# Hybrid attention block: projections in another order, keeping split and later, a third score bank, and key halves copied by DMA

## The chip, the core and the metric

The kernel runs on one core of one Trainium2 chip. The metric is the device time of one execution in microseconds (us); where several executions were timed, their median. TensorE is called PE (PEld is its weight load), VectorE DVE, ScalarE ACT, GpSimd POOL, and SyncE SP. SP issues all the kernel's DMAs.

## What is computed

A decoder trunk of two layers over 512 tokens of width 1024, in float32. Each layer projects its input into fifteen parts for three groups of heads, runs the attention of each group, projects the result back, and then runs a gated MLP with a short convolution.

```python
def fox_attention(q, k, v, log_f):            # 4 heads, causal, S = 512
    ...
        s = jnp.einsum('bqhd,bkhd->bhqk', qb, k) * ATTN_SCALE
        s = s + c_q - c_k                     # c = cumsum(log_f)
        p, _ = masked_softmax(s, kpos[None, :] <= qpos[:, None])
    ...
def nsa_attention(q, kc, vc, ks, vs, kw, vw, gates, ...):   # 8 query heads, 2 key/value groups
    k_cmp = nsa_compress(kc, cmp_pos_k, cmp_w1_k, cmp_w2_k)
    v_cmp = nsa_compress(vc, cmp_pos_v, cmp_w1_v, cmp_w2_v)
    ...
        o = gb[..., 0:1] * o_c + gb[..., 1:2] * o_s + gb[..., 2:3] * o_w
    ...
def dilated_attention(q, k, v):               # 4 heads, three (window, dilation) patterns
    ...
def hybrid_mixer(h, cos, sin, w_in, ...):
    proj = h @ w_in
    (fq, fk, fv, ff, nq, kc, vc, ks, vs, kw, vw, ng, dq, dk, dv) = jnp.split(proj, splits, axis=-1)
    ...
    rope = lambda t, n: partial_rope(heads(t, n), cos, sin)   # nq, kc, ks, kw, dq, dk
    ...
    return mix @ w_out
def conv_ffn(h, w_up, conv_w, conv_b, w_down):
    u = h @ w_up                              # then a causal depthwise convolution of width 3
    ...
    return (jax.nn.silu(a) * b) @ w_down
def reference(x, positions, ...):             # x (1, 512, 1024) float32, 2 layers
    for l in range(DEPTH):
        h = rms_norm(x, attn_pre_norm[l])
        x = x + rms_norm(hybrid_mixer(h, ...), attn_post_norm[l])
        h = rms_norm(x, ffn_pre_norm[l])
        x = x + rms_norm(conv_ffn(h, ...), ffn_post_norm[l])
    return x
```

## The kernel before, in words

**Precision.** Every float32 operand of a matmul is held as two parts, a rounded high part and the rest, both in the type float32r. A product takes three matmuls (high by high, high by low, low by high). So each weight that is loaded is split: `part_weights` lets ACT copy the high part (line 144) and lets DVE (152) or POOL (148, for the names in `ONPOOL`) subtract for the low part. `mm` (line 113) is the helper that issues every matmul except transposes, so one line stands for nearly all of PE's work, and one goes by tile names.

**Weights.** `plan` lists the weight chunks in the order of use. `getw` loads two chunks ahead (`AHEAD`), and splits one ahead (`PRE`) in the attention part. The raw, high and low buffers have three slots each, so the load of a chunk waits on SP until the split three chunks earlier has read its slot, and a split waits until PE has done the chunk three earlier.

**PSUM.** Eight banks of 128x512 float32 carry names: acc (three: projections, compression, output sums), s (two: scores), o (one: attention output), pt (two: transposes). `ps(tag)` takes the next free bank of a name; PE waits at the first matmul into it until the readers of the old tile are done.

**The attention part** is one loop over 96 units plus 7 slots. A unit is one block of 128 queries of one head and branch: 16 units for FoX (group "f"), 64 for NSA ("n", 8 heads by two branches, selected and window, by 4 blocks), 16 for the dilated heads ("d"). Each unit runs through stages at fixed lags (`LAGS`): the score matmuls at lag 0 (`st_scores`), the masked row maximum on DVE (`st_max`, line 1084), the exponential on ACT (`st_exp`, 1089), the normalization on POOL (`st_norm`, 1096), the transposes on PE (`st_turn`, 1107), the split of the transposed block on ACT and DVE (1124, 1129), the value matmuls at lag 7, and the output. Blocks 0 and 1 of a head share one score bank.

**The filler.** Between units the loop calls `step()`, which advances the generator `main_pieces` by one piece: a quarter of a 128-column projection (`projT`, 6 matmuls of 512 columns), an eighth of a 256-column one (`proj256`, 12 matmuls of 256), a quarter of the compression MLP (`hidden`), and so on. The budget is 5 steps ahead of the loop, then 1.4 steps a unit for 12 units, and 0.8 after. `pieces.later(d, fn, ...)` puts work off by d steps. `operands(u)` calls `until(key, n)`: where a unit needs a query or key tile that has not been kept yet, the loop makes steps until it has. PE's order is this program order, written out by hand; the order on the other engines, SP too, is chosen by the framework's scheduler.

**Order of projections before:** kc (two chunks: compression keys and values, turned into windows), ks, sv, nq0 (two chunks, query heads 0 to 3), kw merged with the first compression MLP, nq1 (two chunks, heads 4 to 7) merged with the second, dv, dq, dk, and then the first half of the output projection. `merge(a, b)` takes two pieces of a and one of b in turn.

**Keeping.** One step after a projection chunk ends, `keep` runs `rope`: DVE shuffles the bank and multiplies it by the cosine (464, 465), POOL multiplies by the sine and adds (466, 467). The rotated tile lies in SBUF. `EV[3]` steps later `keep2` makes the operands: for a query pair `q_evac` (ACT 474, DVE 475, twice), for keys `k_evac` (ACT 486 four times, DVE 488 four times). A key tile holds the high part in its first half of columns and the low part in the second, and the same 64 rows twice, in both halves of the partitions; before, ACT and DVE write both copies.

**At the head of a layer** the FoX keys and values are projected (`pk_` holds the keys in two acc banks), then `fq_proj(0)` and `fq_proj(1)`, then the prefix sums of the log forget gates (`pcs`, matmuls with `utri`, line 598), and then the loop begins with kc; all of these use acc banks.

**The compression chain** (`cmp_pieces`) runs beside the loop, one part per unit, from the end of the second compression MLP: it takes banks of the name `CT` for two transposes, for the compressed keys and values, for four score tiles and for four transposes (line 1004).

**The FFN** uses all eight banks by name in turn (`tg`, `dacc`, `X8`).

## Time and profile before

| What | Value |
|---|---|
| Runs shown: lowest, median, highest | 1411.82, 1412.58, 1418.45 us |
| The profiled execution's own time | 1416.81 us |
| Its span, first to last instruction | 1415.0 us |
| Busy: PE, PEld, DVE, ACT, POOL | 94%, 81%, 63%, 51%, 27% |
| Granted clock of TensorE, mean | 0.986 |
| DMA | 123.67 MB, 161962 packets, mean 87 GB/s |

All durations come from the one profiled execution, and times are counted from the start of its span. Busy times are unions of instruction spans. Matmuls are pipelined and their ends are modelled, so the difference of two starts is what one of them took. An idle time before an instruction is given with what ended it, inferred from semaphores. Layer 0's attention loop lies at about 60 to 340 us of the span, layer 1's at about 757 to 1035.

### The profile page before, as it was taken

How to read it: one execution, taken by the hardware profiler on the slowest of the kernel's cores; microseconds unless marked ns; L12 is line 12 of the kernel's file. 1: busy time of each engine (PE TensorE's matmuls, PEld its weight loads, DVE VectorE, ACT ScalarE, POOL GpSimd, SP SyncE). 2: the span in 40 equal slices, each digit the busy share in tenths (PEclk: the TensorE clock that was granted, in tenths of full speed). 3: DMA queues.
4: the chain of work that ended last, by engine and by line, in shares of the span. 5: the costliest groups of instructions: out<-in, count | busy, mean ns of one | idle time of the engine just before them, and what ended most of it. 6: DMA issues, size and time to landing. Idle time of an engine off the chain costs nothing.

```text
span 1415.0 us, 19975 instructions
## 1 busy us (share of the span) xinstructions
PE 1337.1 (94%) x7291; PEld 1151.2 (81%) x7291; DVE 892.9 (63%) x1867; ACT 725.6 (51%) x1469; POOL 377.6 (27%) x409
## 2 busy tenths in 40 slices
PE   6987999998999999999999988989989999999997
PEld 5876887887888888888887878979878888888886
DVE  7767878877655555533476687787686555554334
ACT  5656675775543333332374667677754333333322
POOL 2385576545000000000006657654440000000000
PEclk9999999999999999999999989999999999999999
DMA  6222321123233333323423132202313333323231
GB/s 175 76 60 75 99 71 31 46 75 119 66 99 96 98 96 98 96 98 111 119 90 90 60 105 75 60 31 69 112 60 89 91 103 91 103 91 104 90 120 59
DMA packets 161962, 123.67 MB, mean 87 GB/s; under 512 B 8329, under 2 KB 152137, under 8 KB 161865
## 3 DMA queue, kind: packets, MB, share of 16 engines
q1 hardware_dynamic: 161864, 122.40, 28.8%
q8 instruction: 57, 0.93, 0.3%
q14 instruction: 41, 0.33, 0.1%
HBM read 118.19 MB, written 4.19 MB: 86 GB/s over the span
## 4 chain that ended last, share of the span: by engine, by line
PE 70%; DVE 12%; ACT 7%; POOL 6%; issue 3%; DMA 1%; SPq 0%; POOLq 0%; DVEq 0%; ACTq 0%
PE acc L113 31%; PE s L113 16%; PE pt L113 12%; PE o L113 9%; PE pt L1107 2%; DVE k L488 1%; POOL r L467 1%; DVE q L475 1%; DVE wl_w L152 1%; POOL r L466 1%; ACT r L1089 1%; POOL wt L781 1%; DVE x L308 1%; DVE hl L274 1%; DVE pl L1129 1%
## 5 line engine op out<-in xcount | busy, mean ns | idle before, releaser
L152 DVE TENSOR_TENSOR wl_up<-raw_up,wh_up 128x1024 fp32r<-128x1024 f32 x78 | 95.5, 1225 | 163.2 <-ACT wh_up L144 163.2
L144 ACT ACTIVATE wh_up<-raw_up 128x1024 fp32r<-128x1024 f32 (+1 forms) x90 | 89.4, 1002 | 154.1 <-PE acc L113 67.9
L152 DVE TENSOR_TENSOR wl_wd<-raw_wd,wh_wd 128x1024 fp32r<-128x1024 f32 x42 | 51.5, 1225 | 133.5 <-ACT wh_wd L144 133.5
L113 PE MATMUL s<-k,q 128*128 128x512 f32 (+3 forms) x384 | 100.6, 343 | 23.8 <-DVE sm L1084 8.3
L148 POOL TENSOR_TENSOR wl_kc<-raw_kc,wh_kc 128x512 fp32r<-128x512 f32 x8 | 12.2, 1546 | 411.1 <-ACT wh_kc L144 411.1
L144 ACT ACTIVATE wh_wd<-raw_wd 128x1024 fp32r<-128x1024 f32 x42 | 44.5, 1060 | 144.5 <-PE pt L113 135.5
L1089 ACT ACTIVATE r<-r,sm 128x128 f32<-128x128 f32 x192 | 106.8, 557 | 19.7 <-DVE sm L1084 18.8
L1096 POOL TENSOR_SCALAR r<-r,sm,gates 128x128 f32<-128x128 f32 (+3 forms) x128 | 86.2, 680 | 88.0 <-DVE sm L1094 48.1
L113 PE MATMUL acc<-hh,wh_up 128*128 128x512 f32 (+1 forms) x272 | 102.4, 376 | 0.0
L113 PE MATMUL acc<-hl,wh_up 128*128 128x512 f32 (+1 forms) x272 | 102.4, 376 | 0.0
L113 PE MATMUL acc<-hh,wl_up 128*128 128x512 f32 (+1 forms) x272 | 102.4, 376 | 0.0
L113 PEld LDWEIGHTS s<-k,q 128*128 128x128 f32 x384 | 65.0, 198 | 36.0 <-DVE sm L1084 11.8
L1129 DVE TENSOR_TENSOR pl<-pt,ph 128x384 fp32r<-128x384 f32 x144 | 85.2, 593 | 13.0 <-ACT ph L1124 11.9
L1124 ACT ACTIVATE ph<-pt 128x384 fp32r<-128x384 f32 x144 | 74.4, 518 | 34.9 <-PE pt L1107 33.8
L1107 PE MATMUL pt<-ident,r 128*128 128x128 f32 x480 | 80.1, 283 | 7.7 <-POOL r L1096 4.9
L1084 DVE CUSTOM_DVE_ANT_0 r<-s,cmask 128x128 f32<-128x128 f32 (+3 forms) x160 | 74.8, 481 | 17.4 <-PE s L113 15.3
L113 PE MATMUL acc<-wh_wd,gh 128*128 128x512 f32 x252 | 83.7, 389 | 0.0
L113 PE MATMUL s<-hh,wh_up 128*128 128x512 f32 (+1 forms) x224 | 80.6, 360 | 0.9 <-DVE hl L274 0.9
L113 PE MATMUL s<-hl,wh_up 128*128 128x512 f32 (+1 forms) x224 | 80.3, 359 | 0.0
L113 PE MATMUL s<-hh,wl_up 128*128 128x512 f32 (+1 forms) x224 | 80.3, 359 | 0.0
L113 PE MATMUL o<-ph,v 128*128 128x256 f32 (+1 forms) x288 | 72.8, 279 | 0.8 <-DVE mx L1165 0.8
L113 PE MATMUL o<-pl,v 128*128 128x256 f32 (+1 forms) x288 | 70.0, 290 | 1.7 <-DVE pl L1129 1.7
(434 smaller groups left out, 4023.4 us busy)
## 6 DMA issues: line engine op xcount, KB each, us to landing
raw_up<-in_w_up_dram SPq DMA_DIRECT2D x88, 512.0 KB, 3.8
raw_wd<-in_w_down_dram SPq DMA_DIRECT2D x44, 512.0 KB, 3.4
raw_wo<-in_w_out_dram SPq DMA_DIRECT2D x16, 512.0 KB, 3.5
x<-in_x_dram SPq DMA_DIRECT2D x8, 512.0 KB, 5.7
raw_nq<-in_w_in_dram SPq DMA_DIRECT2D x8, 512.0 KB, 3.8
raw_w<-in_cmp_w_k_dram SPq DMA_DIRECT2D x8, 512.0 KB, 4.0
raw_w<-in_cmp_w_v_dram SPq DMA_DIRECT2D x8, 512.0 KB, 3.8
raw_fk<-in_w_in_dram SPq DMA_DIRECT2D x4, 512.0 KB, 4.8
```

The costliest lines, as they stand in the source:

```text
L113: nc.tensor.matmul(o, lhsT=lhsT, rhs=rhs, start=start, stop=stop, skip_group_check=True)
L144: nc.scalar.activation(hi[:, ks], raw[:, ks], AF.Copy)
L152: nc.vector.tensor_sub(lo[:, ks], raw[:, ks], f(hi)[:, ks])
L274: nc.vector.scalar_tensor_tensor(lo, src, gain[:, k:k + 1], f(hi), op0=ALU.mult, op1=ALU.subtract)
L308: nc.vector.scalar_tensor_tensor(xs[s][:, cs], hs[s][:, cs], stats["r", s // 2][:, j:j + 1], xs[s][:, cs], op0=ALU.mult, op1=ALU.add)
L466: nc.gpsimd.tensor_mul(w, w, sinT)
L1084: nc.vector.tensor_tensor_reduce(row[:, 0:n], u["S"][:, 0:n], u["mask"][:, 512 - n:512], op0=ALU.add, op1=ALU.min, scale=1.0, scalar=3.0e3 ...
L1089: nc.scalar.activation(row[:, 0:n], row[:, 0:n], AF.Exp, scale=-1.0, bias=sm_[:, 0:1], accum_out=sm_[:, 1:2])
L1096: nc.gpsimd.tensor_scalar(row[:, 0:n], row[:, 0:n], sm_[:, 2:3], g_, op0=ALU.mult, op1=ALU.mult)
L1107: nc.tensor.transpose(p[:, 128 * b:128 * b + 128], src, ident)
L1124: nc.scalar.activation(hi, src, AF.Copy)
L1129: nc.vector.tensor_sub(*u["lo"])
```

## The change

Five things are changed together.

- **Order.** nq0 is one chunk now (query heads 0 and 1) and comes, with kw, ahead of sv. nq1 (heads 2 and 3) is merged with the first compression MLP, nq2 and nq3 (heads 4 to 7), one after the other (`both`), with the second. The plan of weights follows.
- **Keeping.** `EV[3]` goes from 1 to 2, and a query or key tile's two halves are made in two different steps.
- **Banks.** acc goes from three to two, s from two to three; where three acc banks were named together, one name becomes s, and the compression chain (`CT`) uses s.
- **Copies.** In `one_k` ACT and DVE write a key tile's rows once, and a DMA on SP's queue copies the 64 rows of 4 KB to the other half of the partitions. The FoX keys (`k_evac`) stay as they were.
- **Rows.** `NROW`, the number of row buffers of 128x512, goes from 10 to 12.

```diff
--- before.py
+++ after.py
@@ -24,22 +24,22 @@
             0.00027424818836152554, 5.3182957344688475e-05, 1.0313385246263351e-05)
 NST = 4
 NBIG = 24
-NROW = 10
+NROW = 12
 LAGS = (1, 2, 4, 5, 7, 7)
 TAIL = 4
-ONPOOL = ("sv", "dv", "dq", "dk", "ks", "nq0", "kw", "kc", "nq1",
+ONPOOL = ("sv", "dv", "dq", "dk", "ks", "nq0", "kw", "kc", "nq1", "nq2", "nq3",
           (0, "fk", 0), (0, "fk", 1), ("up", 0, 1), ("up", 0, 2), ("up", 0, 3), ("up", 1, 0))
 PRE = 1
 HCUT = ((0, 2), (2, 4))
 WGAP = 1
 CL = (1, 3, 5, 6)
-OT = (("acc", "acc"), ("acc", "s"), ("s", "o"), ("acc", "acc"))
+OT = (("acc", "acc"), ("s", "s"), ("s", "o"), ("acc", "acc"))
 PCUT = ((0, 2), (2, 4))
 X8 = "acc"
-CT = "acc"
+CT = "s"
 FIRST = 5
 DCUTS = ("w1", "wo")
-EV = (1, 3, 1, 1)
+EV = (1, 3, 1, 2)
 ORDER = (0, 1, 2, 4, 3, 5, 6, 7, 8)
 GM1 = ((0, 0), (0, 1), (1, 0), (1, 1), (2, 0), (2, 1), (3, 0), (3, 1))
 HA0 = (1, 3)
@@ -87,7 +87,7 @@
     small = ctx.enter_context(tc.tile_pool(name="small", bufs=8))
     psum = ctx.enter_context(tc.tile_pool(name="psum", bufs=1, space=PS))
     dram = ctx.enter_context(tc.tile_pool(name="dram", bufs=1, space=bass.MemoryType.DRAM))
-    PSB = {"acc": 3, "o": 1, "s": 2, "pt": 2}
+    PSB = {"acc": 2, "o": 1, "s": 3, "pt": 2}
     uid = [0]
 
     def nm(p):
@@ -177,15 +177,16 @@
         turned("fq", C_FQ, C_FQ + 128)
         turned("kc", C_KC, C_KC + 128)
         turned("ks", C_KC + 256)
+        turned("nq0", C_NQ)
+        turned("kw", C_KW)
         for c in range(2):
             ks = slice(4 * c, 4 * c + 4)
             plan.append(((l, "sv", c), [(wi[:, ks, C_KC + 384:C_KC + 512], 0, 0), (wi[:, ks, C_KW + 128:C_KW + 256], 0, 128)],
                          4, 256, False))
-        turned("nq0", C_NQ, C_NQ + 128)
-        for kv, starts in enumerate(((C_KW,), (C_NQ + 256, C_NQ + 384))):
+        for kv in range(2):
             for c in range(2):
-                if c < len(starts):
-                    plan.append(((l, ("kw", "nq1")[kv], c), [(wi[:, :, starts[c]:starts[c] + 128], 0, 0)], 8, 128, False))
+                if kv or c == 0:
+                    turned("nq%d" % (1 + kv + c), C_NQ + 128 * (1 + kv + c))
                 for d in range(2):
                     k0 = 8 * c + 4 * d
                     plan.append(((l, "w1", kv, 2 * c + d), [(w1s[kv][:, k0:k0 + 4, :], 0, 0)], 4, 256, False))
@@ -467,26 +468,30 @@
             nc.gpsimd.tensor_add(r, r, w)
             return r
 
+        def q_half(q, p, j):
+            src = p[64 * j:64 * j + 64, :]
+            nc.scalar.activation(q[0:64, j, :], src, AF.Copy, scale=-0.125)
+            nc.vector.scalar_tensor_tensor(q[64:128, j, :], src, -0.125, f(q[0:64, j, :]),
+                                           op0=ALU.mult, op1=ALU.subtract)
+
+        def k_half(k, p, j):
+
+            src = p[64 * j:64 * j + 64, :]
+            for u in (j, 1 - j):
+                nc.scalar.activation(k[64 * u:64 * u + 64, 0, :], src, AF.Copy)
+            for u in (j, 1 - j):
+                nc.vector.tensor_sub(k[64 * u:64 * u + 64, 1, :], src, f(k[64 * j:64 * j + 64, 0, :]))
+
         def q_evac(p):
             q = bt([128, 2, 512], F32R, "q")
             for j in range(2):
-                src = p[64 * j:64 * j + 64, :]
-                nc.scalar.activation(q[0:64, j, :], src, AF.Copy, scale=-0.125)
-                nc.vector.scalar_tensor_tensor(q[64:128, j, :], src, -0.125, f(q[0:64, j, :]),
-                                               op0=ALU.mult, op1=ALU.subtract)
+                q_half(q, p, j)
             return q
 
         def k_evac(p):
-
-            ks = []
+            ks = [bt([128, 2, 512], F32R, "k") for j in range(2)]
             for j in range(2):
-                k = bt([128, 2, 512], F32R, "k")
-                src = p[64 * j:64 * j + 64, :]
-                for u in (j, 1 - j):
-                    nc.scalar.activation(k[64 * u:64 * u + 64, 0, :], src, AF.Copy)
-                for u in (j, 1 - j):
-                    nc.vector.tensor_sub(k[64 * u:64 * u + 64, 1, :], src, f(k[64 * j:64 * j + 64, 0, :]))
-                ks.append(k)
+                k_half(ks[j], p, j)
             return ks
 
         def new_v():
@@ -509,7 +514,7 @@
         row_bcast(bias[:, 4:28], b_nsa_gate[l])
         zz = small.tile([128, NST, 28], F32, tag="zz", bufs=1, name=nm("zz"))
         wv = [getw(l, "fv", c, ahead=1) for c in range(3)]
-        pk_ = [ps("acc"), ps("acc")]
+        pk_ = [ps("acc"), ps("s")]
         fv = [new_v(), new_v()]
         tmode = tc.manual_schedule(engines={mybir.EngineType.PE})
         tmode.__enter__()
@@ -717,10 +722,26 @@
                     yield
 
         def keep(p, key):
-            pieces.later(EV[3], keep2, rope(p), key)
-
-        def keep2(r, key):
-            store.setdefault(key, []).extend([q_evac(r)] if key[-1] == "q" else k_evac(r))
+            r = rope(p)
+            if key[-1] == "q":
+                q = bt([128, 2, 512], F32R, "q")
+                pieces.later(EV[3], q_half, q, r, 0)
+                pieces.later(EV[3] + 1, last_q, key, q, r)
+            else:
+                pieces.later(EV[3], one_k, key, r, 0)
+                pieces.later(EV[3] + 1, one_k, key, r, 1)
+
+        def last_q(key, q, r):
+            q_half(q, r, 1)
+            store.setdefault(key, []).append(q)
+
+        def one_k(key, r, j):
+            k = bt([128, 2, 512], F32R, "k")
+            own, other = (slice(64 * u, 64 * u + 64) for u in (j, 1 - j))
+            nc.scalar.activation(k[own, 0, :], r[own, :], AF.Copy)
+            nc.vector.tensor_sub(k[own, 1, :], r[own, :], f(k[own, 0, :]))
+            nc.sync.dma_start(f(k[other]), f(k[own]))
+            store.setdefault(key, []).append(k)
 
         def sv_evac(s, p):
             if s == 0:
@@ -810,10 +831,11 @@
             pieces.later(3, pos_turn)
             yield from projT("kc", turn=(win_k, win_v))
             yield from projT("ks", "nks")
+            yield from projT("nq0", "nq")
+            yield from projT("kw", "nkw")
             yield from proj256("sv", sv_evac, [])
-            yield from projT("nq0", "nq")
             xc = rt((128, 256))
-            for kv, g in ((0, projT("kw", "nkw")), (1, projT("nq1", "nq"))):
+            for kv, g in ((0, projT("nq1", "nq")), (1, both(projT("nq2", "nq"), projT("nq3", "nq")))):
                 while len(wins.get(kv, ())) < 2:
                     yield
                 yield from merge(g, hidden(kv))
@@ -841,6 +863,10 @@
 
             yield from out_first()
             yield from out_start()
+
+        def both(a, b):
+            yield from a
+            yield from b
 
         def merge(a, b):
 
@@ -1232,7 +1258,7 @@
             pre_h(2, HA1)
             pre_h(3, HA1)
             table(AF.Silu, hs[3][:, 0:1])
-            pts = [ps(t) for t in ("acc", "acc", "s", "s")]
+            pts = [ps(t) for t in ("acc", "s", "s", "s")]
             for half in range(2):
                 if half == 1:
                     turn_pair(1, 1, l, HT3)
@@ -1254,7 +1280,7 @@
         for i in range(11):
             gt = bt([128, 2, 512], name="g")
             gts.append(gt)
-            tg = ("acc", "acc", "s", "s") if i % 2 == 0 else ("pt", "pt", X8, "o")
+            tg = ("acc", "s", "s", "s") if i % 2 == 0 else ("pt", "pt", X8, "o")
             for c in range(2):
                 cd = []
                 for b in range(2):
@@ -1270,7 +1296,7 @@
                 nc.vector.tensor_mul(gt[:, c, :], cd[0], cd[1])
         table(AF.Sqrt, cd[0][:, 0:1])
 
-        dacc = [(ps("acc"), ps("acc")), (ps("s"), ps("s")), (ps("o"), ps(X8)), (ps("pt"), ps("pt"))]
+        dacc = [(ps("acc"), ps("acc")), (ps("s"), ps("s")), (ps("o"), ps("s")), (ps("pt"), ps("pt"))]
         NK = DFF // 128
         dw, gs = {}, {}
```

## Rows read from the trace of the kernel before

**Rows 1.** The page: busy time of the engines with their share of the span and the number of instructions, and the chain of work that ended last, by engine.

```profile
PE 1337.1 (94%) x7291; PEld 1151.2 (81%) x7291; DVE 892.9 (63%) x1867; ACT 725.6 (51%) x1469; POOL 377.6 (27%) x409
...
PE 70%; DVE 12%; ACT 7%; POOL 6%; issue 3%; DMA 1%; SPq 0%; POOLq 0%; DVEq 0%; ACTq 0%
```

**Rows 2.** Busy time of each engine in stretches: one of layer 0's attention loop, and one of its FFN. The columns are the stretch, its length, busy us and instructions of PE, PEld, DVE, ACT and POOL, granted clock, DMA share and GB/s.

```profile
100.00:145.00 45.00, 37.27 (x221) 32.99 (x220) 34.62 (x85) 28.53 (x70) 25.74 (x27) 0.95 0.29 82
...
440.00:600.00 160.00, 160.00 (x707) 132.27 (x706) 88.43 (x104) 60.99 (x76) 0.00 (x0) 1.00 0.32 96
```

**Rows 3.** PE's waits in layer 0's attention loop, 60 to 300 us: who waited for whom, us in total, times, longest us.

```profile
PE s L113 <- DVE sm L1084: 4.2, 4, 1.5
PE s L113 <- ACT k L486: 3.4, 1, 3.4
...
PE pt L1107 <- POOL r L1096: 2.5, 2, 2.3
PE s L113 <- DVE k L488: 2.3, 1, 2.3
PE s L113 <- DVE q L475: 2.1, 1, 2.1
PE pt L1107 <- DVE pl L1129: 1.2, 1, 1.2
```

**Rows 4.** The timeline of PE: scores that had to wait, in layer 0 (78.99 is unit 4, 119.91 unit 16, 138.51 and 141.09 unit 20) and layer 1 (814.49, 834.55, 837.13). Columns: start, length, engine, line, operation, output and inputs, shape, count, and in brackets the idle time before it and what ended it.

```profile
78.99 0.44 PE L113 MATMUL s<-k,q 128*128 128x128 f32 x2 [0.77 <-DVE sm L1084]
...
119.91 0.44 PE L113 MATMUL s<-k,q 128*128 128x128 f32 x2 [2.05 <-DVE q L475]
...
138.51 0.33 PE L113 MATMUL s<-k,q 128*128 128x128 f32 x1 [3.42 <-ACT k L486]
141.09 0.48 PE L113 MATMUL s<-k,q 128*128 128x128 f32 x1 [2.25 <-DVE k L488]
...
165.51 0.73 PE L113 MATMUL s<-k,q 128*128 128x512 f32 x2 [1.50 <-DVE sm L1084]
...
814.49 0.44 PE L113 MATMUL s<-k,q 128*128 128x128 f32 x2 [2.05 <-DVE q L475]
...
834.55 0.33 PE L113 MATMUL s<-k,q 128*128 128x128 f32 x1 [3.30 <-ACT k L486]
837.13 0.47 PE L113 MATMUL s<-k,q 128*128 128x128 f32 x1 [2.25 <-DVE k L488]
```

**Rows 5.** Stretches of PE alone behind the waits of rows 4: length, PE busy with its instructions, granted clock, DMA share, GB/s.

```profile
140.20:146.90 6.70, 5.81 (x26) 0.50 0.49 130
816.10:819.40 3.30, 3.30 (x12) 0.50 0.37 108
836.60:843.30 6.70, 6.17 (x28) 0.50 0.40 112
```

**Rows 6.** ACT's waits for the last rope instruction over the whole kernel (total, times, longest), and one such place in the timeline of ACT.

```profile
ACT q L474 <- POOL r L467: 22.7, 12, 3.0
...
162.84 1.28 ACT L474 ACTIVATE q<-r 64x512 fp32r<-64x512 f32 x2 [3.01 <-POOL r L467]
```

**Rows 7.** The key tiles' instructions from rotated rows: count, shortest, median and longest ns, first and last start, forms.

```profile
L488 DVE TENSOR_TENSOR k<-r,k x32: 675/687/1662, 93.9 to 961.2; 64x512 fp32r<-64x512 f32 x32
```

**Rows 8.** The chain of waits at the head of layer 0's loop (start, length, what).

```profile
66.44 0.63 ACT wh_sv L144
```

**Rows 9.** The head of the loop in the timelines of PE and DVE, layer 0 and layer 1: the first matmul of kc, and the last subtraction of the second FoX query tile.

```profile
60.88 0.47 PE L113 MATMUL acc<-hh,wh_kc 128*128 128x512 f32 x1 [1.07 <-DVE q L475]
...
62.52 0.70 DVE L475 SCALAR_TENSOR_TENSOR q<-acc,q 64x512 fp32r<-64x512 f32 x1 [0.66 <-ACT q L474]
...
755.45 0.47 PE L113 MATMUL acc<-hh,wh_kc 128*128 128x512 f32 x1
...
757.09 0.69 DVE L475 SCALAR_TENSOR_TENSOR q<-acc,q 64x512 fp32r<-64x512 f32 x1 [0.66 <-ACT q L474]
```

**Rows 10.** The emptying of kc's second bank, in the timelines of PE and ACT: the first matmul of ks, ACT's copy of kc's second chunk, and the first two matmuls of sv.

```profile
73.57 0.39 PE L113 MATMUL acc<-hh,wh_ks 128*128 128x512 f32 x1
...
78.82 0.60 ACT L766 ACTIVATE r<-acc 128x512 f32<-128x512 f32 x1
...
82.87 0.28 PE L113 MATMUL acc<-wh_sv,hh 128*128 128x256 f32 x1
82.98 0.28 PE L113 MATMUL acc<-wl_sv,hh 128*128 128x256 f32 x1
```

**Rows 11.** The timeline of PE: the third transpose of the compression chain in layer 0.

```profile
228.11 0.41 PE L1004 MATMUL acc<-ident,r 128*128 128x128 f32 x2 [3.36 <-DVE sm L1094]
```

**Rows 12.** POOL in the stretch from 66 to 118 us: its busy time (then clock and DMA), and one of a rope's two instructions in the groups by line (count, busy us, mean ns, idle before).

```profile
66.00:118.00 52.00, 38.67 (x37) 1.00 0.19 54
...
L466 POOL TENSOR_TENSOR r<-r,sinT 128x512 f32<-128x512 f32 x3 | 3.9, 1292 | 0.0
```

**Rows 13.** The timeline of DVE: three weight subtractions of one shape, two of them in one row.

```profile
160.13 3.22 DVE L152 TENSOR_TENSOR wl_w<-raw_w,wh_w 128x512 fp32r<-128x512 f32 x2
...
165.91 0.67 DVE L152 TENSOR_TENSOR wl_w<-raw_w,wh_w 128x512 fp32r<-128x512 f32 x1
```

**Rows 14.** DMA issues by tile: count, KB each, median us from issue to landing (xsv lies in device memory).

```profile
xsv<-x SPq DMA_DIRECT2D x4, 512.0 KB, 3.4
...
w2r<-in_cmp_w_v_dram SPq DMA_DIRECT2D x2, 64.0 KB, 2.2
```

## The prediction

> **What bounds the kernel now.** I read the page first: PE is busy for 1337.1 of 1415.0 us, nothing else above 63%, and the chain of waits is 70% PE [rows 1]. Then the stretches. In the FFN (440 to 600 us) PE is busy for all 160.00 us, so nothing outside PE's own work can make that part shorter, and the change leaves its matmuls alone. In the attention part it falls short: 37.27 of 45 us [rows 2]. The time to win is there, in PE's waits, so the waits of PE in attention come next [rows 3]. They are few and large: scores waiting for ACT k and DVE k (3.4 and 2.3 us), for DVE q (2.1), and for DVE sm, the row maximum that empties a score bank (4.2 in four waits). The timeline shows where they are: the head's first rotated query at 119.91 (2.05), the window keys at 138.51 and 141.09 (3.42 and 2.25), score banks at 78.99 and 165.51 (0.77 and 1.50); layer 1 repeats them at 814.49, 834.55 and 837.13 [rows 4]. Third, the granted clock: it is 0.50 (1.2 GHz) for 6.7 us behind the waits at 138 to 141, for 3.3 us behind the one at 814, for 6.7 us behind those at 834 to 837, against 1.00 (2.4 GHz) in the FFN [rows 2, 5]. PE is busy through most of these stretches, so half of each is lost: 3.3, 1.6 and 3.3 us.
>
> **Part 1, the order of projections.** A "step" is one turn of the piece generator. The loop has made about 24 steps at unit 16 (5 ahead, 1.4 for each of 12 units, 0.8 after) and 30 at unit 20. Before, kc takes steps 1 to 8, ks to 12, sv to 20, nq0 to 28, and kw, merged with the first compression pieces, ends at 33. So the first NSA unit (16) forces 2 steps until the query is kept, and unit 20, the first with window keys, forces 5 until step 35, and then stands behind rope and keep: the waits of rows 4. After, nq0 is steps 13 to 16 and kw 17 to 20; the keys are kept by step 24. Unit 16 now forces 5 steps for sv, but scores do not read sv, only the values stage seven units on, so PE has work in each forced step and no keep behind it. Removed: 2.05+3.42+2.25 = 7.7 us in layer 0, 2.05+3.30+2.25 = 7.6 in layer 1 [rows 4], and with them the slow clock, 3.3 and 1.6+3.3 [rows 5]: 11.0 and 12.5.
>
> **Part 2, later and halved keeping.** ACT and DVE run in order. Before, a keep is issued one step behind its rope, and ACT stands at it until POOL's last rope instruction: 22.7 us in 12 waits at q over the kernel [rows 6]. At 162.84 that is 3.01 us, followed by two DVE query instructions in one block, with the row maximum behind them, and PE's wait at 165.51 [rows 4]. A step later, and half a tile at a time, the exponentials go ahead. With the third score bank (part 3) I take away the score-bank waits from 165.51 on: the 4.2 of the four less twice 0.77 for the early two, 2.6 a layer (layer 1's the same). For PE's other wait of a keep's kind, DVE pl (1.2 in layer 0 [rows 3]), I take 0.5 a layer, bounds 0 and 1.2. Removed work: each of 16 rotated key tiles loses one ACT copy and one DVE subtraction, the latter 0.687 us: 11 us of DVE time [rows 7]. I cost this at nothing more on the path; it is the cover of the next part.
>
> **Part 3, banks: acc 3 to 2, s 2 to 3.** The score-bank wait at 78.99 and the one before it won't pay: there the chain runs from ACT's weight split at 66.44, whose buffer (one of three) is free when kc's matmuls end [rows 8], over POOL to the normalization that PE awaits for 2.5 us [rows 3], and PE coming earlier would only wait longer. A loss is plain: fq, the prefix sums (utri) and kc follow each other in acc. The sums used a bank of their own; now they need the first fq's, and kc the second's. kc stood for the first query (DVE q) until 60.88; DVE finishes the second at 63.22. In layer 1 kc starts at 755.45, and the second query ends at 757.78 [rows 9]. So kc starts at about 63.3 and 757.9, 2.4 us late in each layer, and the POOL chain of rows 8 starts behind kc, so all of it counts: 4.8. Elsewhere a projection has its bank again two chunks later. The slowest emptying is kc's second: it ends about when ks begins, 73.57, ACT reads it from 78.82 for 0.60, and the second next chunk begins at 82.87 [rows 10]; it holds by 3.4 us. FFN and output banks are renamed one for one: nothing.
> The compression chain moves from acc to s. With its tiles among the scores' three banks, a score can wait for one. The nearest row is PE's wait of 3.36 at a compression transpose, 228.11 [rows 11], which stays, as it waits for data. Bounds 0 and 3.4 a layer; I take 1, since a wait just ahead of 228.11 falls into the one that is there.
>
> **Part 4, POOL.** The ropes of nq0 and kw move from about 115 to 137 us to between 89 and 112. A rope is two instructions of 1.29, 2.6 us of POOL. From 66 to 118 POOL is busy for 38.67 of 52 us with three ropes in it [rows 12]; a fourth, and part of a fifth, make 41 to 44. Bounds: 0, and 5.2 a layer if both stand on the path; I take 2, nearer to the idle time of that row than to a full engine.
> The rows also show DVE slowed beside POOL: two weight subtractions take 3.22 us from 160.13, just where POOL runs the rope that ACT awaits at 162.84 [rows 6], and a lone one 0.67 [rows 13]. The Trainium skill (SBUF — State Buffer, Who interferes with whom) says that a DVE instruction with two SBUF inputs and a GpSimd instruction that reads SBUF exclude each other for a whole instruction; this trace agrees, and the rule speaks against ropes in a fuller stretch. It makes the POOL rival below likelier.
>
> **Part 5, the copies.** Added: 16 DMAs of 256 KB. Nearest rows: 64 KB land in 2.2 us, 512 KB from SBUF in 3.4 [rows 14]; I take 3. The keys are kept 4 units or more before their first score, and a unit takes 3.4 us (unit 4 starts at 78.99, unit 16 at 119.91 [rows 4]): 13 us of cover, so this is hidden. If that cover were gone it would cost 2.2 to 3.4 a tile. SP issues in order and stands for free raw buffers, so a copy can wait there for one, or hold up the loads behind it. Loads are issued two chunks ahead of use and split one ahead, so a chunk, 9.3 us [rows 10], covers the load and such a wait. I cost it at 0; bounds 0 and 3.4 a layer, for the last kept key alone.
> The forced steps for sv need the next weights split sooner: four pieces of 12 matmuls, 0.12 us apart [rows 10], are 5.7 us, against two POOL instructions of about 1.29 [rows 12] behind ACT. 0 to 2 a layer, I take 0.7.
>
> **The sum.** Gains: 11.0+12.5+2x2.6+2x0.5 = 29.7. Losses: 4.8+2x(1+2+0+0.7) = 12.2. Net 17.5 off the profiled execution's 1416.81 us (span 1415.0): 1399.3. That execution lies 4.2 above the median of the runs shown, 1412.58, so a median comes to 1412.58-17.5 = 1395.
>
> **Rivals.** (a) POOL takes the place of the keeps: with the ropes in a full stretch, normalization comes late for units 5 to 16 and the forced steps at 16 end in a wait. For it: PE already waited 2.5 us for POOL there, and rows 13. Against: 13 us of POOL's 52 are idle. Price: upper bounds throughout, 4.8+2x(3.4+5.2+3.4+2) = 32.8 against 29.7: about 1416. The case spans from halfway there to there, 1405 to 1416, middle 1410. (b) Slower: two acc banks are too few. Place: each chunk start in attention. It decides once a chunk's bank is read later than one chunk (9.3 us, 73.57 to 82.87) behind its end; kc's was read 5.9 us behind. With 12 chunks a layer and 2 us each beyond that, 48 us: 1395+48 = 1443; if in half of them, 1419. (c) The change doesn't do what it says: the scheduler issues the halves together and the copies late, so that only part 1 remains: 23.5-12.2 = 11.3 off, 1401. (d) Better: only the 4.8 are lost and keeping pays its bound: 11.0+12.5+5.2+2.4-4.8 = 26.3 off, 1386.
>
> **How the numbers follow.** Forecast 0.57 (own range 1388 to 1405), (a) 0.20, (b) 0.09, (c) 0.08, (d) 0.06. The range from 1383 to 1413 holds all but (b), a part of (a), and what I overlooked. About 0.5% is what a measurement of this kernel can tell from no change, here 1405.5 and 1419.6. Faster: forecast, (c), (d) = 0.71 less a little for their edges, 0.70; same: most of (a) and a little of (b), 0.20; slower: 0.10.
>
> **What would show it.** Right: no PE wait on k or q at the first NSA head's units, clock 1.00 there in both layers; kc starting 2 to 3 us later behind DVE q; no ACT wait of 3 us at a keep; copies landing far ahead of their scores. Wrong: new waits of PE on POOL r between units 5 and 16, matmuls into acc waiting for DVE r, or SP standing at copies while PE waits for weights.

## The result, and the profile after

The changed kernel takes 1425.30 us (median of 6 runs, 1424.59 to 1427.71) beside 1416.78 (1411.82 to 1418.72) of the kernel before in the same comparison: ratio 1.0069, 95% interval 1.0049 to 1.0090. It is 0.7% slower where I forecast 1.2% faster, and above the range. Its profiled execution has a span of 1423.1 us, 8.1 more than before. Two of e6's twelve executions and one of e7's seven, further down, were slow ones of 1655 to 3380 us, and the medians given there are of the others.

The page of the changed kernel, busy time and chain by engine, answers to [rows 1]:

```profile
PE 1339.5 (94%) x7291; PEld 1153.1 (81%) x7291; DVE 881.6 (62%) x1851; ACT 716.5 (50%) x1453; POOL 382.9 (27%) x409
...
PE 66%; DVE 11%; POOL 8%; ACT 8%; issue 5%; DMA 1%; SPq 0%; ACTq 0%; DVEq 0%; POOLq 0%
```

DVE and ACT lost some 11 and 9 us of work, and the chain that ended last has less PE and more POOL, ACT and issue in it. Work went away and waiting came. Who waits is in PE's waits of layer 0's loop, 60 to 310 us (total, times, longest), which answer to [rows 3]:

```profile
PE pt L1133 <- POOL r L1122: 10.2, 5, 4.3
PE pt L1133 <- DVE sm L1120: 3.9, 2, 3.1
PE acc L113 <- DVE q L474: 3.8, 2, 2.7
PE s L1030 <- DVE pcl L1038: 1.9, 1, 1.9
PE acc L113 <- DVE r L466: 1.8, 2, 1.0
PE acc L113 <- DVE v L503: 1.4, 1, 1.4
PE s L1030 <- DVE sm L1110: 1.0, 1, 1.0
```

No score waits for k, q or its bank any more (one transpose of the compression, line 1030, waits 1.0 us for a bank of the scores): what I meant to remove is removed. In its place the transposes (1133) wait for normalized rows (POOL 1122), and matmuls into acc wait for their bank. The places are in PE's timeline, which answers to [rows 4] (start, length, what; in brackets the idle time before and what ended it):

```profile
61.38 0.38 PE L113 MATMUL acc<-utri,lfh 128*4 128x128 f32 x2 [2.66 <-DVE q L474]
63.86 0.67 PE L113 MATMUL acc<-hh,wh_kc 128*128 128x512 f32 x1 [1.17 <-DVE q L474]
91.82 0.90 PE L1133 MATMUL pt<-ident,r 128*128 128x128 f32 x3 [3.80 <-POOL r L1122]
111.54 0.69 PE L1133 MATMUL pt<-ident,r 128*128 128x128 f32 x3 [3.12 <-DVE sm L1120]
131.00 0.47 PE L113 MATMUL acc<-hh,wh_nq 128*128 128x512 f32 x1 [1.43 <-DVE v L503]
192.69 0.55 PE L1133 MATMUL pt<-ident,r 128*128 128x128 f32 x3 [4.28 <-POOL r L1122]
```

Matching the first score of the same unit in both timelines tells where time is won and lost. Start before, and start after less start before, in us:

```
unit            0     4     8    12    24    28    40    44    56    60    92
before, l. 0  68.2  79.0  93.5 106.4 151.2 158.7 187.3 195.9 232.4 242.6 308.9
after, l. 0   +4.6  +2.6  +5.3  +8.4  -3.3  -0.5  -3.0  +2.5  -1.1  +3.6  +4.2
after, l. 1   +7.1  +5.1  +7.9  +9.6  -0.8  +2.0  -0.5  +5.8  +2.3  +6.9  +7.5
```

Units 12 to 24, where the waits of [rows 4] were, win 11.7 us in layer 0 and 10.4 in layer 1 (some 2.7 of each only moved: between these starts stand 11 filler steps of projections against 13 before, 12 matmuls of 512 columns less, 0.23 us from start to start). The head loses 4.6 before unit 0 (2.9 in layer 1, from +4.2 to +7.1), units 4 to 12 lose 5.8 and 4.5, units 24 to 28 lose 2.8 twice, units 40 to 44 lose 5.5 and 6.3, and units 56 to 60, the compression chain, 4.7 and 4.6. Units 44 to 56 win 3.6 and 3.5: PE's wait for the compression, at 228.11 ahead of unit 56 before [rows 11], now falls behind that unit's start. So units 44 to 60 together lose 1.1 in each layer.

The clock follows. These are stretches of the changed kernel, of the form of [rows 2, 5]; the number behind those of POOL is the granted clock:

```profile
64.00:67.40 3.40, 3.40 (x9) 2.62 (x10) 0.42 (x1) 0.00 (x0) 0.00 (x0) 0.50 0.59 154
91.30:94.70 3.40, 2.88 (x9) 2.40 (x10) 3.17 (x14) 2.58 (x9) 3.40 (x5) 0.50 0.60 157
193.70:197.10 3.40, 3.40 (x17) 3.10 (x16) 3.00 (x12) 1.76 (x7) 1.75 (x3) 0.50 0.07 16
890.00:896.80 6.80, 5.45 (x24) 5.15 (x25) 4.92 (x16) 3.25 (x10) 4.03 (x7) 0.50 0.11 31
440.00:600.00 160.00, 160.00 (x706) 132.27 (x706) 88.05 (x105) 61.02 (x75) 0.00 (x0) 1.00 0.32 96
```

At the old place, 140.2 to 146.9, the clock is 1.00 now; it is 0.50 (1.2 GHz) at the new waits instead, those that end at 61.4, 91.8, 192.7 and 891.4, each time after PE had stood. By the mean clock, 0.983 of 1423.1 us beside 0.986 of 1415.0, the slow stretches cost some 24 us in place of 20: an estimate, and about half of the 8.1 us. The FFN's stretch is as it was, 160.00 of 160.

The largest new wait, in units 40 to 44, read across four engines. POOL's timeline from 183.7, then ACT's, then DVE's:

```profile
183.71 1.32 POOL L467 TENSOR_TENSOR r<-r,sinT 128x512 f32<-128x512 f32 x1
184.96 1.32 POOL L148 TENSOR_TENSOR wl_dq<-raw_dq,wh_dq 128x512 fp32r<-128x512 f32 x1
186.21 1.32 POOL L468 TENSOR_TENSOR r<-r,r 128x512 f32<-128x512 f32 x1
187.44 1.32 POOL L148 TENSOR_TENSOR wl_dq<-raw_dq,wh_dq 128x512 fp32r<-128x512 f32 x1
188.69 0.65 POOL L932 TENSOR_TENSOR r<-r 128x256 f32<-128x256 f32 x1
...
191.22 0.72 POOL L938 TENSOR_TENSOR r<-w2r,r 128x256 fp32r<-128x256 f32 x1
191.93 1.45 POOL L1122 TENSOR_SCALAR r<-r,sm,gates 128x384 f32<-128x384 f32 x2
```

```profile
187.56 0.63 ACT L473 ACTIVATE q<-r 64x512 fp32r<-64x512 f32 x1 [3.09 <-POOL r L468]
...
189.18 0.72 ACT L1115 ACTIVATE r<-r,sm 128x512 f32<-128x512 f32 x1
```

```profile
185.37 0.16 DVE L1120 RECIPROCAL sm<-sm 128x1 f32<-128x1 f32 x1
188.23 2.45 DVE L474 SCALAR_TENSOR_TENSOR q<-r,q 64x512 fp32r<-64x512 f32 x2 [2.70 <-ACT q L473]
190.71 0.16 DVE L1120 RECIPROCAL sm<-sm 128x1 f32<-128x1 f32 x1
```

The row sum's reciprocal that PE needs next is ready at 185.53. Its normalization starts at 191.93: for 6.4 us it stands in POOL's queue behind a rope's second half, two weight splits of dq and 3.2 us of the compression's own steps. The rope takes 3.8 us from 183.71 to 187.53, since one of these splits lies between its two instructions. ACT, in order, stands 3.09 us at a query half for it, with an exponential behind that whose maximum DVE had ended at 185.45; DVE stands 2.70 for ACT, and the next reciprocal behind that. So a rope on POOL also holds up ACT, ACT holds up DVE, and DVE feeds POOL. But this second loop reaches only the next row here, whose reciprocal ends at 190.87 and whose normalization follows at 192.62: PE's 4.28 us come from POOL's queue alone.

The same distance can be read for every row: the time from the end of a unit's reciprocal on DVE to the start of its normalization on POOL, the two taken in order. In layer 0, in us (e1 and e13 are runs described below):

```
unit                                  6    11    20    21    22    23    38
before                              0.1   0.5   0.1   0.1   0.2   0.2   0.3
after                               3.7   2.8   3.8   4.1   3.7   2.9   6.4
e1, only the new order              0.1   2.7   3.7   4.1   4.1   2.5   1.1
e13, after with ropes on DVE        0.2   0.1   0.6   0.9   1.2   0.2   1.8
```

PE needs a row five units later, so units 20 to 23 are the waits in units 24 to 28, and 38 the one in units 40 to 44. In e1 the reciprocal of unit 38 comes late itself, 6 us behind its exponential, since DVE stands at the query halves for ACT: there the second loop is seen too.

ACT's waits at a half for the last rope instruction, counted over the whole kernel, answer to [rows 6] (there 22.7 at q; at k it was 11.2 in 6):

```profile
ACT q L473 <- POOL r L468: 24.9, 10, 5.0
ACT k L741 <- POOL r L468: 19.1, 6, 3.5
```

They rose from 33.9 to 44.0 us although the halves are made a step later. (With the new order and the old keeping, e1, they are 44.7.) The copies (page, DMA issues: count, KB, median us to landing) are as estimated:

```profile
k<-k SPq DMA_DIRECT2D x16, 256.0 KB, 2.9
```

### The profile page after: what moved, and what is told of

It reads as the page before. It is cut to its first block, busy times and chain, and to the rows that moved or that the text cites. A ratio compares the mean times of both kernels' runs of the same rounds, so it can differ in the third digit from the quotient of the medians.

```text
span 1423.1 us, 19961 instructions
## 1 busy us (share of the span) xinstructions
PE 1339.5 (94%) x7291; PEld 1153.1 (81%) x7291; DVE 881.6 (62%) x1851; ACT 716.5 (50%) x1453; POOL 382.9 (27%) x409
## 4 chain that ended last, share of the span: by engine, by line
PE 66%; DVE 11%; POOL 8%; ACT 8%; issue 5%; DMA 1%; SPq 0%; ACTq 0%; DVEq 0%; POOLq 0%
PE s L113 23%; PE acc L113 20%; PE pt L113 12%; PE o L113 8%; PE pt L1133 2%; ACT r L1115 2%; POOL r L468 2%; POOL r L467 1%; DVE r L1110 1%; DVE pl L1155 1%; POOL wt L802 1%; POOL r L1122 1%; DVE x L309 1%; DVE hl L275 1%; ACT ph L1150 1%
## 5 line engine op out<-in xcount | busy, mean ns | idle before, releaser
L113 PE MATMUL s<-hh,wh_up 128*128 128x512 f32 (+1 forms) x336 | 120.8, 360 | 1.9 <-DVE hl L275 1.9
L113 PE MATMUL s<-hl,wh_up 128*128 128x512 f32 (+1 forms) x336 | 120.5, 359 | 0.0
L113 PE MATMUL s<-hh,wl_up 128*128 128x512 f32 (+1 forms) x336 | 120.5, 359 | 0.0
L1122 POOL TENSOR_SCALAR r<-r,sm,gates 128x128 f32<-128x128 f32 (+3 forms) x128 | 92.3, 726 | 98.2 <-DVE sm L1120 80.6
L1133 PE MATMUL pt<-ident,r 128*128 128x128 f32 x480 | 82.5, 286 | 29.1 <-POOL r L1122 21.4
L113 PE MATMUL s<-k,q 128*128 128x512 f32 (+3 forms) x384 | 96.7, 334 | 1.0 <-DVE pcl L1038 1.0
L1133 PEld LDWEIGHTS pt<-ident,r 128*128 128x128 f32 x480 | 56.9, 145 | 41.8 <-POOL r L1122 25.5
L113 PE MATMUL s<-wh_wd,gh 128*128 128x512 f32 x252 | 83.9, 390 | 0.0
L113 PEld LDWEIGHTS s<-hh,wh_up 128*128 128x128 f32 x336 | 63.4, 189 | 12.1 <-issue 2.6
L113 PEld LDWEIGHTS s<-k,q 128*128 128x128 f32 x384 | 64.5, 194 | 10.4 <-issue 2.9
L113 PEld LDWEIGHTS s<-hl,wh_up 128*128 128x128 f32 x336 | 63.5, 189 | 9.4
L113 PEld LDWEIGHTS s<-hh,wl_up 128*128 128x128 f32 x336 | 63.4, 189 | 9.2
```

Of the source, the lines that this page charges most:

```text
L113: nc.tensor.matmul(o, lhsT=lhsT, rhs=rhs, start=start, stop=stop, skip_group_check=True)
L1122: nc.gpsimd.tensor_scalar(row[:, 0:n], row[:, 0:n], sm_[:, 2:3], g_, op0=ALU.mult, op1=ALU.mult)
L1133: nc.tensor.transpose(p[:, 128 * b:128 * b + 128], src, ident)
```

## The experiments

After the traces three theories stood. **Banks:** the order's gain was lost to having two acc banks. **POOL:** it was lost in POOL's queue, to ropes and weight splits that stand before the normalization. **Keeping:** it was lost to the halves made later. Each run was compared with the kernel before in its own comparison (medians there 1413.7 to 1415.3). Times are medians; a difference between two changed kernels is taken both directly and by their distances to the kernel before, and given as a span where these differ.

**One part alone or undone.** Four runs first. Their edits are shown in part, with dots where lines are left out.

e1_order_alone, in the kernel before (the plan of weights and the names nq2 and nq3 in `ONPOOL` with it):

```diff
+            yield from projT("nq0", "nq")
+            yield from projT("kw", "nkw")
             yield from proj256("sv", sv_evac, [])
-            yield from projT("nq0", "nq")
...
-            for kv, g in ((0, projT("kw", "nkw")), (1, projT("nq1", "nq"))):
+            for kv, g in ((0, projT("nq1", "nq")), (1, both(projT("nq2", "nq"), projT("nq3", "nq")))):
```

> The kernel before with the new order of projections and nothing else of the change (three acc banks, undivided keeping, no copies). Three theories for the time that the order won at the first NSA head and that the changed kernel lost again. Banks: it was lost to having two acc banks, so the order alone keeps most of its gain, about 1400 to 1406 us beside 1417 of the kernel before. POOL: it was lost to ropes and weight splits that the order puts into a fuller stretch of POOL, so PE's waits for the normalization, 3.8 us in unit 4 to 7 and 3.1 in unit 8 to 11, stand here too, and the time is 1408 to 1414. Keeping: it was lost to the halves made a step later (the 4.3 us wait in units 40 to 43 and the slow clock behind it), so that wait is absent here.

Measured: 1435.48 us, ratio 1.0147 (1.0123 to 1.0171). No theory had this: the order alone loses 21 us. It is ahead of the kernel before by 6.5 us at unit 24 of layer 0, and behind by 0.5 at unit 44, 4.3 at unit 60 and 9.0 at unit 72. PE's waits in layer 0's loop:

```profile
PE pt L1113 <- POOL r L1102: 10.0, 5, 5.1
PE s L113 <- DVE sm L1090: 9.6, 5, 4.1
PE acc L1010 <- DVE sm L1001: 4.8, 1, 4.8
```

The wait for POOL in units 40 to 44 (5.1 us) is here without any of the new keeping, so Keeping falls as the cause of it, and with three acc banks, so Banks falls too.

e2_banks_back, in the changed kernel (and the other names of the diff with it):

```diff
-    PSB = {"acc": 2, "o": 1, "s": 3, "pt": 2}
+    PSB = {"acc": 3, "o": 1, "s": 2, "pt": 2}
```

> The changed kernel with the banks of the one before (acc three, s two, the compression chain in acc). Banks: the head of each layer starts 4.6 and 2.9 us earlier, the waits of matmuls into acc for DVE v (1.4 and 2.4) and DVE r (1.0 and 0.8 a layer) go, the score-bank waits come back (some 2.6 a layer): about 1412 to 1416 us beside 1425. POOL and keeping: only the head's 7.5 come back and the score waits are added, 1420 to 1425, with the 4.3 us wait in units 40 to 43 unchanged.

Measured: 1414.74 us, 0.9995 (0.9981 to 1.0009). Banks' number: 8 to 11 us come back. But that only reaches the kernel before, and the wait in units 40 to 44 is still there (5.2 us). Beside e1, which has the same banks and the old keeping, ACT's waits at halves are no shorter (44.0 and 44.7), but PE waits less for row maxima and for the compression in layer 0 (9.6 and 4.8 in e1):

```profile
PE s L113 <- DVE sm L1110: 6.5, 6, 2.9
PE acc L1030 <- DVE pcl L1038: 2.8, 1, 2.8
```

e3_keep_back, in the changed kernel (its 12 row buffers stay):

```diff
-EV = (1, 3, 1, 2)
+EV = (1, 3, 1, 1)
...
+            pieces.later(EV[3], keep2, rope(p), key)
```

> The changed kernel with the keeping of the one before: both halves in one step, one step behind the rope, key halves copied by ACT and DVE, no copies by DMA. Keeping: the 4.3 us wait in units 40 to 43 and the slow clock behind it go (5.4 and 6.3 us in the two layers), 1412 to 1416 us. Banks and POOL: that wait is POOL's queue and moves at most by a unit; ACT and DVE get their 11 us back, 1423 to 1430.

Measured: 1446.97 us, 1.0232 (1.0210 to 1.0254), outside both. With this order the new keeping is worth 22 to 24 us; Keeping as the cause is finished.

e4_copies_back, in the changed kernel:

```diff
-            nc.scalar.activation(k[own, 0, :], r[own, :], AF.Copy)
-            nc.vector.tensor_sub(k[own, 1, :], r[own, :], f(k[own, 0, :]))
-            nc.sync.dma_start(f(k[other]), f(k[own]))
+            k_half(k, r, j)
```

> The changed kernel with the key halves copied by ACT and DVE again in place of the 16 DMAs; halves and their steps stay. My prediction had the copies at no cost and the removed ACT and DVE work as worth nothing on the path: 1424 to 1428 us beside 1425. If the copies hold up loads on SP or land late, they go and the time falls, below 1422. If the removed 11 us of DVE carried part of the path, the time rises, above 1430.

Measured: 1430.37 us, 1.0117 (1.0098 to 1.0136) beside 1.0069 (1.0049 to 1.0090) of the changed kernel: the DMA copies win 5 to 8 us. The removed ACT and DVE work did carry a part of the path.

**The other three combinations.** e5_banks_alone has in the kernel before only the diff's bank names:

```diff
-    PSB = {"acc": 3, "o": 1, "s": 2, "pt": 2}
+    PSB = {"acc": 2, "o": 1, "s": 3, "pt": 2}
```

> The kernel before with the banks of the changed one and nothing else. With the new order the two acc banks have cost 10.6 us (with the new keeping) and 11.5 us (with the old one). Banks theory: the cost belongs to the banks whatever the order, most of it at the head of each layer (4.6 and 2.9 us): 1421 to 1427 us beside 1414 of the kernel before. Rival, that the cost comes with the order (projections through two banks among the values' burst): only the head's 7.5 less 2 to 4 for the score waits that go, 1416 to 1420.

Measured: 1419.79 us, 1.0036 (1.0023 to 1.0049): 4.5 us lost, the rival's number. By the starts of the units it is lost at the heads, 5.2 us in layer 0 and 2.8 in layer 1; units 44 to 60, with the compression in s, lose nothing.

e6_keep_alone has in the kernel before only the new keep with its copies, and the rows:

```diff
-NROW = 10
+NROW = 12
...
-EV = (1, 3, 1, 1)
+EV = (1, 3, 1, 2)
```

> The kernel before with the new keeping (later, in halves, copies by DMA, 12 row buffers) and nothing else. With the new order that keeping has given back 20.7 us (three acc banks) and 21.7 us (two). If parts add up, it is worth that here too: 1391 to 1396 us. If it pays only where the new order has put the keeps and the ropes into one another's way, 1406 to 1416 beside 1414 of the kernel before, with PE's waits for k and q at the first NSA head at least as long as before, since the keys come a step or two later there.

Measured: 1418.07 us, 1.0016 (1.0003 to 1.0028), 2 us above even the second range. Parts do not add up. Here a copy is on the path, since the window keys are kept at the last moment. SP's and PE's timelines:

```profile
139.12 3.98 SPq L742 DMA_DIRECT2D k<-k  x2
```

```profile
142.75 0.66 PE L113 MATMUL s<-k,q 128*128 128x128 f32 x2 [4.71 <-DMA k<-k]
```

From the first copy's issue to the score are 3.6 us.

e7_order_back has in the changed kernel the old order:

```diff
+            yield from proj256("sv", sv_evac, [])
             yield from projT("nq0", "nq")
-            yield from projT("kw", "nkw")
-            yield from proj256("sv", sv_evac, [])
...
-            for kv, g in ((0, projT("nq1", "nq")), (1, both(projT("nq2", "nq"), projT("nq3", "nq")))):
+            for kv, g in ((0, projT("kw", "nkw")), (1, projT("nq1", "nq"))):
```

> The changed kernel with the old order of projections; banks, keeping and copies stay. If parts add up, the order cost 20 us and the time falls to 1402 to 1407. If order and keeping pay only together, it stays at 1417 to 1427, with the waits for k and q at the first NSA head back (2 to 4 us each, three a layer).

Measured: 1422.72 us, 1.0051 (1.0033 to 1.0068): 1 to 3 us under the changed kernel. Eight cases together, us over the kernel before:

```
                    old order   new order
old keeping, 3 acc      0         +21.4
old keeping, 2 acc     +4.5       +32.9
new keeping, 3 acc     +2.8        +0.6
new keeping, 2 acc     +7.5        +8.5 (the change)
```

The new order costs 21 to 28 us with the old keeping and nearly nothing with the new one; the banks cost 4 to 12 for either order and keeping. (The change was compared with a median of 1416.78; beside the 1413.7 to 1415.3 of the other comparisons its 8.5 would be 10 to 12. The old keeping with two acc banks and the new order, e3, has 12 row buffers and not 10, which was not tried by itself.) Banks cannot be the whole: without their cost the new order and keeping together still win nothing.

**What holds the normalization.** e8_three_banks_later takes e2's version and

```diff
-EV = (1, 3, 1, 2)
+EV = (1, 3, 1, 3)
```

> New order, new keeping and copies with the three acc banks of before, and the halves of a key or query made three and four steps behind the rope in place of two and three. Theory: the waits of PE for the normalization (3.0 to 4.0 us in units 8 to 11, 5.2 in units 40 to 43, in each layer) come from ACT and DVE standing at a half for the rope that POOL has not ended, its two instructions being apart by a weight split, and one step more lets the maxima and exponentials go ahead: ACT's 44 us of waiting at halves falls below 25 and the time from 1414.7 to 1400 to 1408. Rival: POOL itself is behind (its weight splits and ropes, whoever waits for them), then the waits stay and the time is 1412 to 1418.

Measured: 1412.81 us, 0.9981 (0.9968 to 0.9993). The rival's number: another step takes ACT's waits at halves from 44.0 to 39.6 us and the time down by 2 to 3, and the wait in units 40 to 44 stays (4.9). My theory that the step is what matters fell; POOL's queue was left, tried in two ways on this version. e9_splits_off_pool:

```diff
-ONPOOL = ("sv", "dv", "dq", "dk", "ks", "nq0", ...
+ONPOOL = ("dk", "ks", "nq0", ...
```

> The version with new order and keeping, three acc banks and halves one step later still (1412.8 us), and the weight splits of sv, dv and dq on DVE in place of POOL. Theory POOL queue: the normalization that PE awaits in units 40 to 43 (4.9 us) had its row sums 6 us before POOL came to it, behind splits of dq, the rope's second instruction and the compression's own steps; without the splits, which stand between the rope's two instructions as well, that wait and the one in units 8 to 11 (2.6 us) fall below half, and the time to 1400 to 1408. Rival, that the keeping on ACT and DVE is what holds the normalization: the waits stay, DVE has 20 more instructions of 0.7 us, 1412 to 1420.

Measured: 1399.51 us, 0.9893 (0.9873 to 0.9912). e10_rope_on_dve:

```diff
-            nc.gpsimd.tensor_mul(w, w, sinT)
-            nc.gpsimd.tensor_add(r, r, w)
+            nc.vector.tensor_mul(w, w, sinT)
+            nc.vector.tensor_add(r, r, w)
```

> The same version (1412.8 us) with both POOL instructions of every rope on DVE, the splits left on POOL. Theory POOL queue: POOL loses 2.6 us for each of the ropes and ACT no longer stands at a half for POOL (39.6 us over the kernel), the waits of PE for the normalization in units 8 to 11, 24 to 27 and 40 to 43 fall below half: 1398 to 1408. Rival, DVE as the bound: some 1.4 us of DVE for each rope on the path of the row maxima, PE waits for DVE in place of POOL, 1414 to 1425.

Measured: 1393.02 us, 0.9845 (0.9820 to 0.9869), the fastest here. Both end below the ranges of POOL's theory, e9 by 0.5 us and e10 by 5, and far below their rivals. PE's waits in layer 0's loop, of e8, e9 and e10 in this order:

```profile
PE pt L1133 <- POOL r L1122: 9.7, 6, 4.9
PE s L113 <- DVE sm L1110: 4.8, 4, 2.6
```

```profile
PE s L113 <- DVE sm L1110: 6.5, 7, 1.5
PE pt L1133 <- POOL r L1122: 5.8, 7, 2.3
```

```profile
PE s L113 <- DVE sm L1110: 4.5, 3, 3.1
PE pt L1133 <- POOL r L1122: 4.5, 3, 3.1
```

e10 has no wait for POOL in units 40 to 44 any more; a wait of 3.1 for a row maximum stands at unit 40 (174.33), and the one for POOL in units 4 to 8 (3.1) is left. e9 shows what the splits had done: there the rope of that place goes through POOL in 2.7 us (3.8 above), with no split between its two instructions:

```profile
173.84 1.27 POOL L467 TENSOR_TENSOR r<-r,sinT 128x512 f32<-128x512 f32 x1 [2.09 <-DVE r L465]
175.30 1.28 POOL L468 TENSOR_TENSOR r<-r,r 128x512 f32<-128x512 f32 x1 [0.19 <-DVE r L466]
```

In e10 ACT waits at halves for a rope 11.8 us in all:

```profile
ACT q L473 <- DVE r L468: 8.3, 2, 4.1
...
ACT k L741 <- DVE r L468: 3.5, 4, 1.1
```

**The head by itself.** e11_sums_in_o, in the changed kernel:

```diff
-        pcs = ps("acc")
+        pcs = ps("o")
```

> The changed kernel with the prefix sums at the head of a layer in the output bank, which is free there, in place of an acc bank; all else as changed (two acc banks). It prices my term of 4.8 us for the head by itself: PE's waits for DVE q (2.7 and 1.2 in layer 0, 1.1 and 1.2 in layer 1) and the slow clock behind them go, 4.6 + 2.9 = 7.5 us: 1417 to 1420 us beside 1425. Rival, that POOL's chain behind kc sets the time there, whatever the head does: the normalization's wait in units 4 to 7 (3.8 us) grows by what is won and 1422 to 1426 remain.

Measured: 1417.79 us, 1.0029 (1.0017 to 1.0041): 4 to 7.5 us. By the starts of unit 0 the head gives back 4.6 us in layer 0 and 2.4 in layer 1, 7.0 together, and units 4 to 16 take a part of it.

**Whose gain it is.** The same rope edit in three other kernels: e12_before_rope_on_dve, e13_after_rope_on_dve, e14_order_rope_on_dve (the edit of e10 in the kernel before, the changed kernel, and e1).

> The kernel before with both POOL instructions of every rope on DVE and nothing else: the control for the same edit, which gave 19.8 us in the version with new order and keeping. Theory, that the new order is worth its gain once POOL is out of the way: the ropes bind less here, PE's waits for k and q at the first NSA head shrink by the rope's 2.6 to 4 us on POOL but do not go, 1404 to 1412 us. Rival, that ropes on POOL cost any order the same: 1392 to 1398, and the new order is worth nothing.

Measured: 1411.08 us, 0.9974 (0.9960 to 0.9989): 3.2 us, at the upper end of the theory's range: PE's wait for the window keys at unit 20 grew from 3.4 to 5.0.

> The changed kernel with both POOL instructions of every rope on DVE and nothing else. POOL queue: the normalization's waits in units 8 to 11, 24 to 27 and 40 to 43 (3.1, 2.1 and 4.3 us) fall below half, the bank waits at the head (4.6 and 2.9) stay: 1403 to 1410 us beside 1425. Rival, that with two acc banks the emptying by DVE now comes late behind the ropes: 1412 to 1425, with PE waiting for DVE at acc banks.

Measured: 1396.70 us, 0.9874 (0.9854 to 0.9893): 26 to 29 us off the changed kernel, more than POOL's theory expected. PE's waits in layer 0's loop:

```profile
PE pt L1133 <- POOL r L1122: 6.0, 4, 3.3
PE acc L113 <- DVE q L474: 3.7, 2, 2.7
PE pt L1133 <- DVE sm L1120: 2.3, 2, 2.0
```

> The kernel before with the new order (1435.5 us) and both POOL instructions of every rope on DVE: three acc banks, undivided keeping one step behind the rope. If it is the rope on POOL that ACT and DVE stood for at the keeps, the loss of 20 us turns into a gain here without the new keeping: 1395 to 1410. If undivided keeping is itself the cost, in length of its block on ACT and DVE, 1418 to 1435.

Measured: 1403.97 us, 0.9928 (0.9911 to 0.9944). The order that cost 21.4 us with ropes on POOL wins 7.1 beside e12 with ropes on DVE, with the old keeping in both. And the whole change, with ropes on DVE in both kernels (e13 beside e12), wins 14.4 us.

e15_after_three_mends puts e10's edit into the changed kernel, and

```diff
-EV = (1, 3, 1, 2)
+EV = (1, 3, 1, 3)
...
-        pcs = ps("acc")
+        pcs = ps("o")
```

> The changed kernel, two acc banks and three score banks, with three edits: ropes on DVE, the prefix sums in the output bank, and halves one step later. Sum of the single effects in us: about 18 to 20 for the ropes, 7.5 for the sums, 2 for the step: 1396 to 1400. Beside 1393.0 for the three acc banks with ropes on DVE it tells what a third score bank is worth: below 1391 if score waits (10.0 us there) bound it, above 1395 if the two acc banks do.

Measured: 1394.19 us, 0.9857 (0.9837 to 0.9877), between the two bounds that I had set for the third score bank, so it is worth nothing that can be told, and 2 us below the sum that I had expected. The effects don't add: beside e13 the head gives 4.9 and 4.0 us by the starts of unit 0, and units 40 to 44 take 3.6 back in each layer (waits for POOL r, 2.2 where e13 has 1.7, and for DVE pl, 1.0).

## Why the prediction was wrong

**Part 1 (order): its place right, its size near, its use not.** Units 12 to 24 win 11.7 and 10.4 us where I had 11.0 and 12.5; less the 2.7 that only moved, 9.0 and 7.7. What I did not see is that the units behind would give it back: e1 is ahead at unit 24 and behind at unit 60, and e14 stays ahead with the ropes off POOL. The pause at the old waits was not one in which POOL caught up: in the kernel before it takes the rows of units 16 to 23 within 0.2 us of their reciprocals, so it was not behind. In the changed kernel those of units 20 to 23 stand 2.9 to 4.1 us, because other work lies in front of them in its queue.

**Part 4 (POOL): the step that failed.** I took 2 us a layer, bounds 0 and 5.2, from two ropes moved and a busy share. The rope edit is worth 26 to 29 us in the changed kernel and 3.2 in the one before, so ropes on POOL cost the change 23 to 25 us, some 12 a layer. With them on DVE in both kernels the change is a gain, 14.4 us, where the sum without Part 4 is 21.5. Two errors lie in it. I read POOL's busy time, which hardly differs (23.45 of 30 us from 170 to 200, and 25.11 before); what counts is the order of its queue, where a row stood 6.4 us, and who stands for it. A rope takes 3.8 us there, not 2.6, when a split lies between, and ACT and DVE, in order, wait in turn. And I looked at one stretch, 66 to 118 us, though the change shifts every later rope against weight splits and compression: units 24 to 28 and 40 to 44 were outside it.

**Part 2 (later keeping): right to want, wrong in the account.** "The exponentials go ahead" failed: ACT's waits at halves rose from 33.9 to 44.0 us, and the new order alone (44.7 in e1) or the new keeping alone (42.6 in e6) does as much; a further step (e8) took only 4.4 of them away. Yet with the new order the keeping wins 20.8 us, so that sum of waits is not its price; in layer 0 it is seen in shorter waits of PE for row maxima and the compression (e2). Alone it loses 2.8. I had 6.2, as a sum of separate parts.

**Part 3 (banks): right, undersized.** The head was to lose 4.8 us and lost 7.5 (7.0 in e11). kc follows the second query as I had it, 0.15 us behind its end at 63.71, but that end itself came 0.5 us later than before, and I left out the slow clock behind it, half of the 3.4 us from 64.0. That score banks would not pay before unit 8 was right: 2.0 us won by unit 4 went into the wait that grew from 2.28 to 3.80. Inside the loop I had acc banks at nothing, since kc's emptying held by 3.4 us; three matmuls a layer wait for theirs, 0.8 to 2.5 us each, 3.2 in layer 0 and 4.2 in layer 1. Rival (b) was wrong by its price and its count. The term of 1 us for the compression's banks agrees with the 1.1 that units 44 to 60 lose, but e2, with the compression back in acc, loses 1.4 and 1.3 there, so this is luck.

**Part 5 (copies): right on the time to land (2.9), on the cover, and near on the price without it** (bounds 2.2 to 3.4; 3.6 to the score in e6). Wrong that the removed work was worth nothing: 5 to 8 us (e4).

**Rival (a)** had the mechanism, POOL in place of the keeps, but its upper bounds ended at 1416; of the signs that I had named, new waits on POOL r and matmuls into acc waiting for DVE r came. SP did stand at the copies for their data, but no wait of PE for weights came of it:

```profile
SPq L743 <- DVE k L742: 36.7, 16, 6.1
```

With some 24 us for the 4 of Part 4, and 7.5 for the 4.8 of the head, the sum turns from 17.5 off to 5 on; 8.5 were measured. That checks the size only, since parts do not add here. The Trainium skill's rule (SBUF — State Buffer, Who interferes with whom), which I had put behind this rival, agrees with DVE's query halves, grouped by form in the changed kernel (shortest, median, longest ns):

```profile
L474 DVE SCALAR_TENSOR_TENSOR q<-r,q x24: 684/797/1655, 109.6 to 949.3; 64x512 fp32r<-64x512 f32 x24
```

The two at 188.23 took 2.45 us beside POOL, where two of the shortest take 1.37. These 1.1 us are no part of the 6.4 that PE's row stood, which were over POOL's own queue; its rope and split instructions there took 1.32 us each, hardly more than the shortest, 1.28. Over the whole kernel no run separates the two, since e9 and e10 both take work off POOL.

What stays open: why the framework's scheduler put the half ahead of the ready exponential on ACT, and the splits between a rope's two instructions; no run changed that order by itself. How e9's splits divide into the three names was not tried, nor the compression's bank names or the row buffers by themselves.

## What to carry to other kernels

A wait that is taken from the busiest engine can come back some units on: before it is counted as gain, follow each of the other engines through the next units with its queue in order, and ask which instruction the path then finds standing behind what. Where a small job goes from engine to engine (here DVE, POOL, ACT, DVE), its delay holds the queues that it stands in and not only its instructions (3.8 us for 2.6), and moving it to one engine can be worth more than balancing busy time. Parts of a change that touch the same queues must be tried in combination: here one alone lost 21 us, one lost 3, and both together nothing.
